# A decoder layer on one core: one table of steps from the opening to the first gate and up products, and 72 products of the output projection behind the last head

## The chip, the cores and the metric

One core of one Trainium2 chip runs the whole layer. The metric is the time of one execution on the device in microseconds (us). The kernel before took 670.38 us, the median of three runs (669.57 to 671.45).

## The reference, cut to what matters

One layer, 512 positions of 1,024 columns, float32:

```
h  = x + rms(mix(rms(x)))                 # sandwich norms around both parts
y  = h + rms(down(silu(gate) * up))       # gate, up = two products of rms(h)

mix: one input projection of rms(x) gives q, k, v of both head groups
  A, 4 heads D0..D3: a = softmax(q1 k1) - lam * softmax(q2 k2);  o = rms(a v)
  B, 8 heads N0..N7 in 2 groups: o = g0 * compressed + g1 * selected + g2 * window
     compressed: 31 blocks of 32 positions, through a small two-layer net
     selected, window: causal softmax over 512 keys
  output projection: concat(A, B) (512 x 1024) times wo (1024 x 1024)
```

The feed-forward part has 2,816 columns, in 22 tiles of 128.

## The kernel before

Every float32 operand of a large product is split in a rounded high part and the rest (whi and wlo, xh and xl, pth and ptl, oh and ol). A product of two such operands is three products on TensorE (PE): high by high, low by high, high by low. ScalarE (ACT) writes most high parts, VectorE (DVE) subtracts most low parts, GpSimd (POOL) some.

The projections (`fm`, `dv`, `vg` in the trace) write q, k and v; q and k go to a scratch in DRAM and come back a head at a time (`qst`, `kst`). A head does, for each of its two maps or branches: score products in three groups of row tiles (`sc`, widths of 128 to 512 columns), maximum on DVE (L510), exponential on ACT (L511), a scaling of the rows (POOL, DVE and ACT, L530 to L534), transposes in three groups (`tr`, L521), high part on ACT (L525), low part on DVE (`ptl`, L526), value products (`av`, `avn`). A differential head (D) then norms its output (`ms`, `rr`, `rs`, `rsb`, L577 to L590). A head of group B (N) adds its compressed branch (`scc`, `pc`, `pcs`, `trc`, `pct`) head by head, in tiles of 128 columns.

The output projection makes four row tiles by two halves of 512 columns, each with three products for each of the eight blocks k of heads: 192 products. `mix_part` (L691) sums the blocks `MIX_A`, which are D0, D1 and N0 to N3, for all four tiles early and parks the sums (`mixp`, 96 products, copied by ACT at L701). `mix_final` (L703) adds the blocks `MIX_B`: for tiles 0 and 1 beside and right behind the last head, for tiles 2 and 3 after that.

Then come the norms (`mixt`, `u`, `x`, a list of short steps `STEPS`, L75, run by `n_step`, L975), their transposes (`trh`, L1020), and the first halves of the first two feed-forward tiles (`gu`, L854), on the rows of tiles 0 and 1. `ff_gate` for the second halves starts when tiles 2 and 3 are normed too; from there on the rest of the feed-forward part (`gw`, L874), the down projection (`acc`, L1166) and the last norm run.

What sets the order: a scheduler places all instructions by simulated times of its own; `ORDER` (L48) is the order in which the projections, heads and weights are written, and heads have a high priority (L545, L549), so that they run above what stands ahead of them. In the norms alone ACT and DVE are held to the written order (`q`, L953). PSUM is split in tags: "mm" 2 banks (projections, mix), "sc" 3 (scores), "tr" 2 (transposes), "av" 1 (values); these are closed behind the heads, and the norms and gates open banks of their own.

Of the kernel before, what the change touches and what calls it, by code (L numbers as in the profile page):

```python
# [46 lines left out]
FIRST_PAIR = {"C": KCVC, "q0": DQ0, "k0": DK0, "n0": NQ0, "s": KSKW, "q1": DQ1, "k1": DK1, "n1": NQ1}  # L47
ORDER = (  # L48
    "C v1 q1 q0 k1 cv n1 W0 k0 n0 ck s v0 g W4 D0 D1 W1 N0 N1 N2 N3 W5 N4 W2 W3 N5 D2 M0 N6 W6 W7 M1 M2 M3 D3 F0 F1 N7"
# [3 lines left out]
PSB = {"mm": 2, "sc": 3, "tr": 2, "av": 1}  # L53
MIX_A = (0, 1, 4, 5)
MIX_B = (2, 3, 6, 7)
# [12 lines left out]
USE_W = "4"  # L68
# [6 lines left out]
STEPS = (  # L75
# [17 lines left out]
def hybrid_block_kernel(  # L93
# [6 lines left out]
    act, dve, pool, pe = nc.scalar, nc.vector, nc.gpsimd, nc.tensor  # L100
# [8 lines left out]
    def load_w(src, w=1024):  # L109
        raw = wpool.tile([P, 1024], F32, tag="raw", name="wraw", bufs=WB[0])  # L110
        nc.sync.dma_start(raw[:, :w], src)
        return raw
# [56 lines left out]
    vcs = T.tile([P, GROUPS, HEAD_DIM], F32R, bufs=1, name="vcs")  # L169
# [18 lines left out]
    nc.sync.dma_start(gc, gcol)  # L188
    xh, xl = [], []
    raws = {}  # L190
    sqs = [None, None]

    def warm(n):
        for j in range(n):
            pe.matmul(warm_ps, warm_b[:, :P], warm_b, start=True, stop=True)

# [3 lines left out]
    warm(WARM)  # L200
# [4 lines left out]
    xraws = [None] * (NK // 2)  # L205

    def load_x(k):
        if k % 2 == 0:
            xraws[k // 2] = T.tile([P, 2, SEQ], F32R, tag="k", name="xraw", bufs=BUFS["k"])
        t = f32(xraws[k // 2][:, k % 2])  # L210
        nc.sync.dma_start(t, xT[:, k])
        h = sslot(f"xh{k}")
        act.activation(h, t, AF.Copy, scale=gc[:, k:k + 1])
        xh.append(h)
        if 0 < k < 4:
            for _ in range(WARMX):
                pe.matmul(warm_ps, h[:, :P], h, start=True, stop=True)

    def low_x(k):
        t = f32(xraws[k // 2][:, k % 2])  # L220
        l = sslot(f"xl{k}")
        dve.scalar_tensor_tensor(l, t, gc[:, k:k + 1], f32(xh[k]), OP.mult, OP.subtract)
        xl.append(l)

    def load_fm(m, split=False):
        raws[m] = load_w(wf[m])
        if split:
            raws[m] = split_w(raws[m])

    first = 2 * FIRST_PAIR[ORDER.split()[0]]  # L230
    load_x(0)
    load_fm(first, True)
    for k in range(1, 4):
        load_x(k)
    load_fm(first + 1, True)
    for k in range(4, NK):
        load_x(k)
    for k in range(NK):
        low_x(k)
    for k in range(NK):  # L240
        t = f32(xraws[k // 2][:, k % 2])
        act.activation(t, t, AF.Square)
        if k < 2:
            sqs[k] = t
        else:
            dve.tensor_tensor(sqs[k % 2], sqs[k % 2], t, OP.add)

    cst = tslot("cst", tag="o")
    nc.sync.dma_start(cst, consts)
    dve.tensor_copy(ident, cst[:, 0:P])  # L250
    dve.tensor_copy(ident_r, cst[:, 0:P])
    dve.tensor_copy(ident_b, cst[:, 0:P])
    dve.memset(mask_b[:, :SEQ - P], 0.0)
    dve.tensor_copy(mask_b[:, SEQ - P:], cst[:, P:2 * P])
    dve.tensor_copy(cmask_b, cst[:, 2 * P:3 * P])
    n2 = GROUPS * NPAD
    dve.tensor_tensor(sel, ident[:, :n2], ident[:, n2:], OP.add)
    for r in (NCMP, n2 + NCMP):
        dve.tensor_tensor(sel, sel, ident[:, r:r + 1].to_broadcast([P, n2]), OP.add)
    dve.tensor_copy(valid, cst[:, 3 * P + 2 * NCMP:3 * P + 2 * NCMP + 1])  # L260
    dve.memset(ones, 1.0)
    zero = T.tile([P, GROUPS], F32, bufs=1, name="zero")
    dve.memset(zero, 0.0)
    rp = [sslot(n, F32) for n in ("cos", "sin", "ckv", "skv")]
    cos, sin, ckv, skv = rp
    for j in range(4):
        nc.sync.dma_start(rp[j], rope[:, j])

    ssum = ps("tr", "ssum")
    for i in range(NT):  # L270
        for j in range(2):
            pe.matmul(ssum[:, i:i + 1], sqs[j][:, i * P:(i + 1) * P], ones, start=(j == 0), stop=(j == 1))
    ssum = ssum[:, :NT]
    rsqrt_mean(rstd, ssum, 1.0 / D_MODEL)
    dve.tensor_scalar_mul(nrstd, rstd, -1.0)
    rb = ps("tr", "rb")
    for i in range(NT):
        pe.matmul(rb[:, i * P:(i + 1) * P], rstd[:, i:i + 1].to_broadcast([P, P]), ident, start=True, stop=True)
    hp = P // 2
    for t in (ckv, skv, cos, sin):  # L280
        dve.tensor_tensor(t, rb, t, OP.mult)

    lv = sslot("lv", F32)
    nc.sync.dma_start(lv[:, :4 * HEAD_DIM], lamv.partition_broadcast(P))
    l2 = T.tile([P, 2], F32, bufs=1, name="l2")
    for j in range(2):
        dve.tensor_tensor(lv[:, 256 + 64 * j:320 + 64 * j], lv[:, 128 * j:128 * j + 64],
                          lv[:, 128 * j + 64:128 * j + 128], OP.mult)
        dve.tensor_reduce(l2[:, j:j + 1], lv[:, 256 + 64 * j:320 + 64 * j], AX.X, OP.add)
    act.activation(l2, l2, AF.Exp)  # L290
    dve.tensor_tensor(lam, l2[:, 1:2], l2[:, 0:1], OP.subtract)
    dve.tensor_scalar_add(lam, lam, -LAM_INIT)


    def fm_tile(m):
        hi, lo = raws.pop(m)
        pt = ps("mm", f"fm{m}")
        seq = [(hi, xh), (lo, xh), (hi, xl)]
        n = 0
        for w, xx in seq:  # L300
            for k in range(NK):
                pe.matmul(pt, w[:, k * P:(k + 1) * P], xx[k], start=(n == 0), stop=(n == 3 * NK - 1))  # L302
                n += 1
        return pt

    def rope_pair(pair, scale, c=None, s=None):
        c = cos if c is None else c
        s = sin if s is None else s
        wide = rope_tile()
        t2, t1, b, a = (f32(wide[:, j]) for j in range(4))  # L310
        for half, outs in enumerate((((t1, c), (a, s)), ((t2, s), (b, c)))):
            m = 2 * pair + half
            if m not in raws:
                load_fm(m, True)
            pt = fm_tile(m)
            if pair == KCVC:
                raw = f32(sslot("craw"))
                act.activation(raw, pt, AF.Copy)
                pt = raw
            for o, tab in outs:  # L320
                dve.scalar_tensor_tensor(o, pt, scale, tab, OP.mult, OP.mult)
        return wide, a, b, t1, t2

    def qk_pair(pair, scale):
        wide, a, b, t1, t2 = rope_pair(pair, scale)
        dve.tensor_tensor(t1, t1, t2, OP.subtract)
        dve.tensor_tensor(a, a, b, OP.add)
        d = dram.tile([4, HALF, 4, SEQ], F32, name=f"qk{pair}")
        hi1, lo1, hi2, lo2 = (wide[:, j] for j in range(4))
        hq = "d" if pair in HIQ else "a"  # L330
        to_r(hq, hi1, t1)
        to_r(hq, hi2, a)
        dve.tensor_tensor(lo1, t1, f32(hi1), OP.subtract)
        dve.tensor_tensor(lo2, a, f32(hi2), OP.subtract)
        nc.sync.dma_start(d.rearrange("m d c t -> (m d) c t"), f32(wide))
        return d

    def load_q(d, m):
        q = T.tile([P, SEQ], F32R, tag="q", name="qst", bufs=BUFS["q"])
        nc.sync.dma_start(f32(q), d[m].rearrange("d c t -> (d c) t"))  # L340
        return q

    def load_k(d, m):
        kk = T.tile([P, 2, SEQ], F32R, tag="k", name="kst", bufs=BUFS["k"])
        src = d[m].rearrange("d (c h) t -> (d c) (h t)", h=2)
        dst = f32(kk).rearrange("(x r) h t -> r x (h t)", r=2)
        for r in range(2):
            nc.sync.dma_start(dst[r], src)
        return kk

    def cmp_pair():
        _, a, b, t1, t2 = rope_pair(KCVC, 1.0, ckv, skv)
        de = f32(rope_tile())[:, :2].rearrange("p x (y n) -> p x y n", y=2)
# [1043 lines left out]
```

## Time and profile before

| what | value |
|---|---|
| time, median of 3 runs | 670.38 us |
| time of the profiled execution | 670.32 us |
| its span in the profile | 668.5 us |
| PE busy | 640.7 us, 96% |
| DVE busy | 559.3 us, 84% |
| ACT busy | 388.6 us, 58% |
| POOL busy | 76.4 us, 11% |

The span is what the profile covers; the time holds 1.8 us around it. A matmul's record lasts until its result has drained, so records of successive products overlap: two products of 0.39 us may start 0.23 us apart, and the spacing is the price of one. "x144" is a count of records, and `128*128 128x512` are the weights' and the moving operand's shape. What stands behind "<-" in brackets is the instruction that ended the wait before a row. In a table of windows the granted clock of PE (1.00 is full) stands behind POOL.

### The profile page before, as it was taken

To read this page: it belongs to the slowest core of one execution; us is meant where nothing else is said; L and a number is where in the kernel's file an instruction comes from. 1 tells how busy PE (TensorE), PEld (TensorE's weight loads), DVE (VectorE), ACT (ScalarE), POOL (GpSimd) and SP (SyncE) were. 2 spreads that over 40 slices of the span, in tenths; PEclk is the share of its full clock that TensorE was granted. 3 is DMA by queue.
4 is the path that set the end of the run, shared out by engine and by line. 5 is a ranking of instruction groups with operands and counts; after the bars stand their busy time and mean duration, and the time that the engine had idled before them with its cause. 6 is when DMAs were issued, how large, how long until landed. Compare 5 with 4: busy or idle time off the path is not lost.

```text
span 668.5 us, 11185 instructions
## 1 busy us (share of the span) xinstructions
PE 640.7 (96%) x4099; PEld 573.1 (86%) x4099; DVE 559.3 (84%) x1114; ACT 388.6 (58%) x820; POOL 76.4 (11%) x86
## 2 busy tenths in 40 slices
PE   8999999999899998888899999999999999999995
PEld 5988788899778787777898999999999998888884
DVE  4878797897999987768999998888888639999966
ACT  6443453657799766635646555555555547665424
POOL 0000000020755532501100000000000000000023
PEclk9999999999999999979989999999999999999998
DMA  8445767771030530136213323323223217562443
GB/s 307 163 142 204 270 223 280 273 284 56 17 127 18 173 104 24 64 106 241 96 64 126 126 97 114 108 96 122 99 95 127 96 49 251 189 219 96 172 112 126
DMA packets 29735, 94.50 MB, mean 141 GB/s; under 512 B 3824, under 2 KB 4720, under 8 KB 28784
## 3 DMA queue, kind: packets, MB, share of 16 engines
q1 hardware_dynamic: 29104, 92.74, 39.5%
q0 software_dynamic: 576, 1.05, 0.9%
q8 instruction: 32, 0.52, 0.3%
q14 instruction: 23, 0.19, 0.1%
HBM read 80.66 MB, written 12.06 MB: 139 GB/s over the span
## 4 chain that ended last, share of the span: by engine, by line
PE 48%; DVE 3%; ACT 1%; issue 1%; DVEq 0%; ACTq 0%
PE gw L874 28%; PE acc L1166 17%; PE gu L854 4%; DVE mixt L958 1%; DVE rr L958 1%; DVE x L958 1%; DVE htl L958 0%; ACT junkb L958 0%; ACT rr L958 0%; ACT hth L958 0%; DVE ug L1073 0%; ACT L859 0%; DVE ffl L1073 0%; DVE cy L930 0%; DVE u L958 0%
## 5 line engine op out<-in xcount | busy, mean ns | idle before, releaser
L530 POOL TENSOR_TENSOR p<-p,l 128x384 f32<-128x384 f32 (+3 forms) x60 | 49.2, 848 | 130.3 <-DVE l L560 57.3
L116 ACT ACTIVATE whi<-wraw 128x1024 fp32r<-128x1024 f32 (+2 forms) x36 | 37.0, 1038 | 44.1 <-PE fm L302 16.0
L511 ACT ACTIVATE p<-p,nm 128x128 f32<-128x128 f32 (+1 forms) x96 | 53.2, 556 | 15.5 <-DVE nm L510 14.9
L126 DVE TENSOR_TENSOR wlo<-wraw,whi 128x1024 fp32r<-128x1024 f32 (+2 forms) x36 | 42.9, 1197 | 18.8 <-ACT whi L116 18.8
L510 DVE CUSTOM_DVE_ANT_0 p<-sc,mask_b 128x128 f32<-128x128 f32 (+1 forms) x96 | 43.9, 483 | 6.5 <-PE sc L506 5.8
L526 DVE TENSOR_TENSOR ptl<-tr,pth 128x384 fp32r<-128x384 f32 (+1 forms) x60 | 35.7, 596 | 5.9 <-ACT pth L525 5.2
L525 ACT ACTIVATE pth<-tr 128x384 fp32r<-128x384 f32 (+1 forms) x60 | 30.9, 517 | 15.4 <-PE tr L521 14.9
L1248 POOL DMA_DIRECT2D rope<-dp x4 | 3.7, 1127 | 315.8 <-DVE rope L1243 315.8
L521 PE MATMUL tr<-ident,p 128*128 128x128 f32 x200 | 34.4, 290 | 3.7 <-DVE rr L139 2.2
L505 PE MATMUL sc<-kst,qst 128*128 128x128 f32 (+2 forms) x96 | 33.5, 357 | 3.9 <-DVE nm L510 2.8
L302 PE MATMUL fm<-xh,whi 128*128 128x512 f32 x128 | 33.5, 396 | 1.2 <-ACT whi L116 1.2
L302 PE MATMUL fm<-xh,wlo 128*128 128x512 f32 x128 | 32.6, 390 | 0.0
L521 PEld LDWEIGHTS tr<-ident,p 128*128 128x128 f32 x200 | 25.2, 149 | 8.6 <-DVE ptl L526 2.9
L302 PE MATMUL fm<-xl,whi 128*128 128x512 f32 x128 | 32.3, 389 | 0.0
L506 PE MATMUL sc<-kst,qst 128*128 128x128 f32 (+2 forms) x96 | 31.0, 326 | 0.0
L302 PEld LDWEIGHTS fm<-xh,whi 128*128 128x128 f32 x128 | 23.6, 188 | 7.0 <-ACT whi L116 1.9
L302 PEld LDWEIGHTS fm<-xl,whi 128*128 128x128 f32 x128 | 24.0, 188 | 5.0
L302 PEld LDWEIGHTS fm<-xh,wlo 128*128 128x128 f32 x128 | 23.8, 188 | 4.8
L505 PEld LDWEIGHTS sc<-kst,qst 128*128 128x128 f32 x96 | 18.5, 193 | 7.7 <-DVE nm L510 6.0
L1073 ACT ACTIVATE ah<-ff 128x256 fp32r<-128x256 f32 (+1 forms) x28 | 14.4, 513 | 14.6 <-DVE ff L1073 11.2
L930 DVE TENSOR_TENSOR cy<-gw,cy 128x512 f32<-128x512 f32 x19 | 13.0, 686 | 11.5 <-PE gw L874 11.5
L874 PE MATMUL gw<-rope,whi 128*128 128x256 f32 x160 | 22.0, 280 | 0.0
(353 smaller groups left out, 2030.3 us busy)
## 6 DMA issues: line engine op xcount, KB each, us to landing
wraw<-in_wg SPq DMA_DIRECT2D x22, 512.0 KB, 3.2
dr<-in_wd SPq DMA_DIRECT2D x22, 512.0 KB, 3.2
wu<-in_wu SPq DMA_DIRECT2D x19, 512.0 KB, 3.2
wraw<-in_wf SPq DMA_DIRECT2D x16, 512.0 KB, 4.7
qk<-rope SPq DMA_DIRECT2D x7, 1024.0 KB, 4.9
kst<-qk SPq DMA_DIRECT2D x24, 256.0 KB, 3.6
qst<-qk SPq DMA_DIRECT2D x16, 256.0 KB, 3.1
wraw<-in_wo SPq DMA_DIRECT2D x8, 512.0 KB, 3.2
```

Of the source, the lines that this page charges most:

```text
L116: act.activation(dst, src, AF.Copy)
L126: (lo_eng or dve).tensor_tensor(lo[:, :w], raw[:, :w], f32(hi[:, :w]), OP.subtract)
L302: pe.matmul(pt, w[:, k * P:(k + 1) * P], xx[k], start=(n == 0), stop=(n == 3 * NK - 1))
L505: pe.matmul(sv, lhs, kk[:, 0, :w], start=True, stop=False)
L506: pe.matmul(sv, lhs, kk[:, 1, :w], start=False, stop=True)
L510: dve.tensor_tensor_reduce(pt, sv, mask_b[:, (NT - 1 - i) * P:], -1.0, BIG, OP.add, OP.min, nm)
L511: act.activation(pt, pt, AF.Exp, bias=nm, scale=-1.0, accum_out=l[:, i:i + 1])
L521: pe.transpose(tr[:, n * P:(n + 1) * P], pts[i][:, j * P:(j + 1) * P], ident)
L526: dve.tensor_tensor(ptl[:, sl], trv, f32(pth[:, sl]), OP.subtract)
L530: pool.tensor_tensor(p, p, l.to_broadcast(list(p.shape)), OP.mult)
L874: m = pe.matmul(pt, ww[:, k * P:(k + 1) * P], hx[k], start=(start and n == 0), stop=(n == 11), skip_group_check=True)
L1166: m = pe.matmul(pt, x, y, start=(start and n == 0), stop=(stop and n == 2), skip_group_check=True)
```

## The change

The instructions from the first load of x to the first halves of the gate products are no longer placed by the scheduler. There are 31 generators ("streams"): loads of x, its high parts, its low parts, weights, projections, evictions, the compression net, scores, maxima, exponentials, scalings, transposes, highs, lows, values, outputs, the differential heads' norms, the output projection's weights, its products, the products behind the last head, four streams of norms, the gates, and so on. A table of 1,543 letters runs the next step of the stream of each letter, and every instruction so issued keeps its written place on its engine:

```diff
-ORDER = (
-    "C v1 q1 q0 k1 cv n1 W0 k0 n0 ck s v0 g W4 D0 D1 W1 N0 N1 N2 N3 W5 N4 W2 W3 N5 D2 M0 N6 W6 W7 M1 M2 M3 D3 F0 F1 N7"
-)
+PROJ = "C v1 q1 k1 cv n1 ck s g q0 k0 v0 n0"
+HEADS = "D2 D3 N4 N5 N6 N7 D0 D1 N0 N1 N2 N3"
+WORDER = "2 3 6 7 0 1 F0 4 5 F1"
+TABLE = (
+    "aaabbcaabbaaPcbPbcbaPaPbaaPbabcPPPPaaccPcPbPbPPPbPPbPcbPPcPdPbdcdPbPPcPbcPSPbcPcPPPPcPPPPcedPPPSSSSeePeP"
...
+    "xxwwwNxNxxNxNWWWWNNNyWWyNyNNzyyzFFyyzFyzyFFzzzzyyyFFyzyzyFzyWzzzzyWFyyzzyyFzzzyyyzFzzFz"
+)
-PSB = {"mm": 2, "sc": 3, "tr": 2, "av": 1}
-MIX_A = (0, 1, 4, 5)
-MIX_B = (2, 3, 6, 7)
+PSB = {"mm": 2, "sc0": 1, "sc1": 1, "sc2": 1, "tr": 2, "av": 1}
+PARK = {1: (2, 3, 6, 7), 2: (2, 3), 3: (2, 3)}
+LATER = {0: (2, 3, 6, 7, 0, 1, 4, 5), 1: (0, 1, 4, 5), 2: (6, 7, 0, 1, 4, 5)}
+LAST_N = 3
+K_LAST = 5
+LATE_PS = {"mix2": ("tr", "tr"), "mix3": ("av", "sc0"), "trh0": ("mm", "mm"), "trh1": ("sc1", "sc2"), "trh2": ("mm", "mm"),
+           "trh3": ("sc1", "sc2"), "gu0": ("tr", "tr"), "gu1": ("av", "sc0")}
-USE_W = "4"
+USE_W = "6"
+    class Written:
+        def __getattr__(self, name):
+            def issue(*a, **k):
+                r = getattr(self.eng, name)(*a, **k)
+                for x in r if isinstance(r, tuple) else (r,):
+                    if self.begun:
+                        tc.keep_in_program_order(x)
+                    self.begun = True
+                return r
+            return issue
+    act, dve, pool, pe, sp = (Written(e) for e in (act, dve, pool, pe, sp))
...
+    need = {t: next(g) for t, g in streams.items()}
+    for t in TABLE:
+        need[t] = next(streams[t], "end")
```

The heads run in the order D2, D3, N4 to N7, D0, D1, N0 to N3; the last block is then k = 5. Row tile 0 parks nothing and sums all its products in PSUM, tile 1 parks the blocks 2, 3, 6, 7, tiles 2 and 3 only 2 and 3. The other six blocks of tiles 2 and 3, 72 products, are a stream (letter N) behind the last head:

```diff
+    def rest():
+        for k in LATER[2]:
+            for i in (2, 3):
+                for c in range(2):
+                    yield [("oh", K_LAST), ("oh", k), ("wo", k)]
+                    if k == LATER[2][0] and not c:
+                        mixes[i] = pair_ps(f"mix{i}")
+                    mix_mul(mixes[i][c], i, c, k, k == LATER[2][0], k == LATER[2][-1])
```

The norms' transposes and the gates use the heads' banks again (`LATE_PS`) and open none of their own. The compressed branch is done for four heads of a group at once, in tiles of 512 columns; the scalings of a head's two branches share one reciprocal and one product with the gates:

```diff
-        def row_scale(b):
-            dve.reciprocal(l[:, b], l[:, b])
-            dve.tensor_tensor(l[:, b], l[:, b], gates[:, :, 3 * h + b], OP.mult)
+                dve.tensor_tensor(l, l, gates[:, :, 3 * h + 1:3 * h + 3].rearrange("p i b -> p b i"), OP.mult)
+                dve.reciprocal(l, l)
-        dve.tensor_reduce(nm, sv, AX.X, OP.max, negate=True)
-        c = T.tile([P, P], F32, tag="pc", name="pc", bufs=2)
+            nm, l = (T.tile([P, nh], F32, tag="nmc", name="nmc", bufs=4) for _ in range(2))
+            dve.tensor_reduce(nm, sv, AX.X, OP.max, negate=True)
+            c = tslot("pc", tag="c")
```

There are 24 loads of `qst` instead of 16, since the compressed scores load their queries apart. The warm products on x are three instead of nine; the products of the first two projections take x in the order of its arrival (`OPEN`). The second feed-forward tile's weights (F1) are split by ACT (high) and POOL (low) instead of DVE, and the norms of the four row tiles are four streams (`NSTEPS`) with the same steps as `STEPS`. From the second halves of the gates on the code is the same.

Two places in PE's program follow. All instructions that the table issues have one line, 230, in the changed kernel; a name's number tells its buffer.

The first place is where the projections end. Before, the last product of the last projection (`vg`) is row 866 of 2,367 of PE's program, with the norm and the scores of a head behind it:

```order
L398 MATMUL vg_1404<-whi,xl_185 128x280
L398 MATMUL vg_1404<-wlo,xh_166 128x280
L398 MATMUL vg_1404<-wlo,xh_169 128x280
L585 MATMUL rsb<-ident,rs 128x128 x4
L505 MATMUL sc<-kst,qst 128x256
L506 MATMUL sc<-kst,qst 128x256
L505 MATMUL sc<-kst,qst 128x512
L506 MATMUL sc<-kst,qst 128x512
L572 MATMUL av<-pth,dv_1212 128x512 x2
L572 MATMUL av<-ptl,dv_1212 128x512
```

In the changed program the last projection (`fm`) ends at row 922 of 2,260, and the head's products stand between its products one by one:

```order
L230 MATMUL fm_2046<-xh_160,wlo 128x512
L230 MATMUL sc<-kst,qst 128x384 x2
L230 MATMUL ms<-ones,sq 128x1 x4
L230 MATMUL tr<-ident,p 128x128 x3
L230 MATMUL av<-pth,vn_1099 128x512
L230 MATMUL av<-ptl,vn_1099 128x512
L230 MATMUL fm_2046<-xh_167,wlo 128x512
L230 MATMUL fm_2046<-xh_173,wlo 128x512
L230 MATMUL fm_2046<-xh_177,wlo 128x512
L230 MATMUL fm_2046<-xh_195,wlo 128x512
```

The first score product moves from row 530 to row 386, so more of the heads' rows stand ahead of the last projection product: before, 140 score, 180 transpose and 172 value products are behind it, after 98, 140 and 139.

The second place is behind the last head, where tiles 2 and 3 of the output projection (`mix`) meet the transposes of the norms of tiles 0 and 1 (`trh`). Before:

```order
L708 MATMUL mix<-ws_2583,oh_3323 128x512
L708 MATMUL mix<-ws_3087,oh_2746 128x512
L708 MATMUL mix<-ws_3087,ol_2747 128x512
L708 MATMUL mix<-ws_3089,oh_2746 128x512
L708 MATMUL mix<-ws_3097,oh_3537 128x512
L708 MATMUL mix<-ws_3097,ol_3538 128x512
L708 MATMUL mix<-ws_3099,oh_3537 128x512
L1020 MATMUL trh<-ident,mixt 128x128 x16
L854 MATMUL gu<-hth,whi 128x256 x16
```

After, in the changed program:

```order
L230 MATMUL mix_3461<-ws_2881,oh_3167 128x512
L230 MATMUL mix_3461<-ws_2881,ol_3168 128x512
L230 MATMUL mix_3461<-ws_2883,oh_3167 128x512
L230 MATMUL trh_3565<-ident,mixt 128x128 x4
L230 MATMUL mix_3462<-ws_2882,oh_3167 128x512
L230 MATMUL mix_3462<-ws_2882,ol_3168 128x512
L230 MATMUL mix_3462<-ws_2884,oh_3167 128x512
L230 MATMUL trh_3566<-ident,mixt 128x128 x4
```

Before, all products of the mix stand ahead of the transposes; after, 39 of the 72 do, and the other 33 stand between and behind the groups of four transposes.

More of the change, by code (lines that the diff above doesn't have):

```diff
@@ L199, in hybrid_block_kernel @@
     warm_ps = ps("av", "warm")
-    warm(WARM)
+    for _ in range(WARM):
+        pe.matmul(warm_ps, warm_b[:, :P], warm_b, start=True, stop=True)
     def rope_tile():
         return R.tile([P, 4, SEQ], F32R, tag="rope", name="rope")
[L205 to L237, printed above, removed]
@@ L273, in hybrid_block_kernel @@
[L273 to L285, printed above, removed]
@@ L306, in rope_pair @@
[L306 to L336, printed above, removed]
+    obj = {}
@@ new lines, in weights @@
+    def weights():
+        todo = [c for tok in PROJ.split()[1:] for c in chunks(tok)]
+        loaded = []
+        for n, (key, src, w) in enumerate(todo):
+            while len(loaded) < min(n + 3, len(todo)):
+                yield ("room", len(loaded))
+                loaded.append(load_w(*todo[len(loaded)][1:]))
+            yield ("room", n)
+            hi, lo = split_slots()
+            act.activation(hi[:, :w], loaded[n][:, :w], AF.Copy)
+            yield
+            dve.tensor_tensor(lo[:, :w], loaded[n][:, :w], f32(hi[:, :w]), OP.subtract)
+            obj[key] = hi, lo
+            obj[("wl",) + key[1:]] = True
@@ new lines, in turned @@
+    def turned():
+        for tok in HEADS.split():
+            if tok[0] == "N":
+                h = int(tok[1])
+                yield ("cgs", h // HPG)
+                tr = ps("tr", "trc", F32R)[:2 * NPAD]
+                for i in range(NT):
+                    b = cgs[h // HPG][h % HPG // 2][:, h % 2 * NT + i].rearrange("p s n -> p (s n)")
+                    pe.transpose(tr[:, i * P:(i + 1) * P], b, ident_r)
+                yield
+                pct = tslot("pct", F32R, "c")[:2 * NPAD]
+                act.activation(pct, f32(tr), AF.Copy)
+                obj["pct", h] = pct
@@ new lines, in hybrid_block_kernel, with transposes @@
+    mats = [(tok, br) for tok in HEADS.split() for br in range(1 if tok[0] == "D" else 2)]
+    def transposes():
+        for mat in mats:
+            for js in GROUPED:
+                yield ("a",) + mat
+                tr, n = ps("tr", "tr"), 0
+                for j in js:
+                    for i in range(j, NT):
+                        pe.transpose(tr[:, n * P:(n + 1) * P], obj[("a",) + mat][i][:, j * P:(j + 1) * P], ident)
+                        n += 1
+                obj["tr", mat, js[0]] = tr[:, :n * P].rearrange("p (j q) -> p j q", q=P)
@@ new lines, in w_col @@
+    def w_col(w, k):
+        if isinstance(w, list):
+            w, k = w[k // 4], k % 4
+        return w[:, k * P:(k + 1) * P]
+    streams = {"a": x_loads(), "b": x_highs(), "c": x_lows(), "d": constants(), "e": row_factors(), "S": weights(), "P": projections(), "R": evictions(), "K": compression(), "G": compressed(), "T": turned(),
+               "Q": loads(), "A": scores(), "X": maxima(), "E": exponentials(), "Y": scalings(), "Z": transposes(),
+               "H": highs(), "L": lows(), "V": values(), "O": outputs(), "J": heads(), "W": out_weights(),
+               "M": mixes_(), "U": parked(),
+               "B": switch(), "N": rest(), "w": norms(0), "x": norms(1), "y": norms(2), "z": norms(3), "F": gates_()}
```

1338 lines of the change are left out of this document (808 added, 530 removed), and 8 rows, old and new, of tables (NSTEPS, STEPS).

## The prediction, made before the changed kernel ran

> **What bounds the kernel now.** I read the page's busy shares first, then a table of windows cut where the program changes stage, then the chain that ended last, and last the PE rows of the weakest window.
>
> ```profile
> PE 640.7 (96%) x4099; PEld 573.1 (86%) x4099; DVE 559.3 (84%) x1114; ACT 388.6 (58%) x820; POOL 76.4 (11%) x86
> ...
> 0.00:20.00 20.00, 18.07 (x69) 11.39 (x70) 10.21 (x23) 13.94 (x22) 0.20 (x4) 1.00 0.85 311
> 20.00:64.00 44.00, 43.77 (x252) 38.33 (x251) 35.50 (x65) 16.77 (x26) 0.00 (x0) 1.00 0.44 142
> 64.00:111.00 47.00, 45.50 (x229) 38.45 (x227) 38.01 (x56) 20.85 (x28) 0.53 (x1) 1.00 0.73 264
> 111.00:164.00 53.00, 52.58 (x373) 49.89 (x374) 44.00 (x112) 32.74 (x87) 4.81 (x6) 1.00 0.62 220
> 164.00:304.00 140.00, 127.50 (x778) 108.74 (x777) 119.51 (x362) 99.80 (x277) 56.94 (x63) 0.96 0.26 84
> 304.00:335.60 31.60, 27.97 (x182) 24.34 (x180) 28.51 (x68) 20.57 (x59) 5.14 (x4) 1.00 0.39 150
> 335.60:550.00 214.40, 213.85 (x1741) 211.15 (x1741) 179.15 (x256) 118.01 (x207) 0.00 (x0) 0.99 0.30 103
> 550.00:668.50 118.50, 111.50 (x485) 90.84 (x485) 104.36 (x180) 65.96 (x117) 8.73 (x8) 0.98 0.49 165
> ```
>
> PE (TensorE) is the bound nearly everywhere. The columns of a window are its length, the busy time of PE, weight load, DVE, ACT and POOL, the granted clock and the DMA. From 335.6 on PE is busy 213.85 of 214.4 us, and nothing the change touches is there: those 332.9 us stay. Before it, two windows are loose: 164 to 304 (the attention heads and the output projection) with 12.5 us without PE, and 304 to 335.6 (the norms and the first gate products) with 3.6. There DVE is the rival bound, at 119.51 of 140 and 28.51 of 31.6.
>
> A busy PE isn't a full one, since records overlap while they drain. So I price products by their spacing:
>
> ```profile
> 335.57 24.34 PE gu L854 x144
> 359.91 187.61 PE gw L874 x1584
> 550.06 111.52 PE acc L1166 x485
> ...
> 283.23 1.05 PE L580 MATMUL ms<-ones,sq 128*128 128x1 f32 x8 [1.26 <-ACT sq L577]
> 292.03 0.34 PE L649 MATMUL avn<-pth,vn 128*128 128x384 f32 x1
> 292.38 0.28 PE L649 MATMUL avn<-pth,vn 128*128 128x256 f32 x1
> 292.61 0.22 PE L649 MATMUL avn<-pth,vn 128*128 128x128 f32 x1
> 292.78 0.40 PE L653 MATMUL avn<-pct,vcs 128*64 128x512 f32 x1
> 293.02 0.49 PE L521 MATMUL tr<-ident,p 128*128 128x128 f32 x3
> 301.94 1.19 PE L708 MATMUL mix<-ws,oh 128*128 128x512 f32 x4 [1.37 <-ACT oh L116]
> 315.68 1.03 PE L1020 MATMUL trh<-ident,mixt 128*128 128x128 f32 x8
> 333.57 0.63 PE L1020 MATMUL trh<-ident,mixt 128*128 128x128 f32 x4 [1.40 <-DVE mixt L958]
> ```
>
> A 512-wide product costs 111.52/485 = 0.230, a 256-wide one 187.61/1584 = 0.118. Two 384-wide ones start 292.03 to 292.38: 0.175 each. Two 128-wide ones start 292.61 to 292.78: 0.085. A score or value product of the heads is a quarter each of these four widths: 0.152. Transposes: 1.03 for eight less 0.63 for four is 0.10; 1.03/8 with the drain is 0.13; I take 0.11. Narrow products: at most 1.05/8 = 0.13; I take 0.115.
>
> Now the weak window by these prices:
>
> ```profile
> L521 PE MATMUL tr<-ident,p 128*128 128x128 f32 x180 | 31.0, 292 | 3.7 <-DVE rr L139 2.2 <-DVE ptl L526 1.5
> L505 PE MATMUL sc<-kst,qst 128*128 128x128 f32 (+2 forms) x70 | 25.1, 368 | 3.1 <-DVE nm L510 2.8
> L649 PE MATMUL avn<-pth,vn 128*128 128x512 f32 (+1 forms) x64 | 20.7, 328 | 0.3 <-DVE opair L661 0.2
> L696 PE MATMUL mixp<-ws,oh 128*128 128x512 f32 x48 | 17.8, 401 | 0.0
> L708 PE MATMUL mix<-ws,oh 128*128 128x512 f32 x30 | 9.9, 399 | 1.4 <-ACT oh L116 1.4
> L598 PE MATMUL scc<-kcl,qst 128*128 128x32 f32 x28 | 6.5, 263 | 0.0
> L585 PE MATMUL rsb<-ident,rs 128*128 128x128 f32 x26 | 4.6, 326 | 1.6 <-DVE rs L146 1.6
> L580 PE MATMUL ms<-ones,sq 128*128 128x1 f32 x24 | 3.0, 245 | 1.3 <-ACT sq L577 1.3
> ```
>
> With the sister rows (L506, L598 and so on are the other parts of a split product), the program has in it 149 512-wide products (mixp 96, mix 45, pct 8) for 34.3 us, 304 score and value products for 46.2, 212 transposes for 23.3 and 106 narrow ones for 12.2: 116 of 140 us. **23.8 us are lost there**, 16% of the time. 5.1 of them are the norm of a differential head (rr 2.2, rs 1.6, sq 1.3), which stands late in the program. From 20 to 164 the same prices leave 3.4 us lost of 144 (2.4%; 2.15 of it idle). From 0 to 20 the 69 products are worth 15.9, so 4.1 are lost. Lost to 304.0 in all: 31.3, and PE's work to there is 272.7.
>
> The Trainium skill's "Perfetto Trace Analysis", section "Identifying the Most-Contended Engine", says that matmul busy time is a poor measure of how near PE is to its limit, and wants weight load's busy share instead. By that share, 86%, 95 us would be free over the whole span. The trace speaks against taking it so here: from 20 to 64 PE runs without a gap at 38.33 of 44, 87%, so that share is what a full PE shows with these products.
>
> **The change, part by part.** *Fewer products.* PE's program is the same but for six warm products fewer (x, 9 to 3): 6 x 0.230 = 1.4. They run while x arrives (DMA 0.85 busy in 0 to 20), so the bounds are 0 and 1.4; I take 1.4, because the new order places real products between the arrivals.
>
> *The output projection's products.* Its 192 products stay. Before, 138 stand ahead of the point where tile 0's mix is done (304.0); after, 114. So 24 x 0.230 = 5.5 leave that part and join the next one.
>
> *Heads beside projections.* The first score product moves from row 530 of PE's program to row 386, and the last projection product from 866 to 922. PE's work by stage is then 71.4 to the first score, 105.8 from there to the last projection, 85.0 on to the last head's values, 3.5 to the join: 265.7. Before, 116 of such work stood with no projection beside it; after, 88.5. This is the main term. Before, heads above projections lose little (0.42 idle of 53 in 111 to 164), because a projection product waits for nothing; so I give the first 176.9 of heads and projections a loss of 3%: 5.3. For the last 88.5 the bounds are 3% and what that window lost without the head's norm, (23.8 - 5.1)/116.2 = 16.1%; the differential heads now stand ahead of four plain heads, and DVE has less to do, but 48 instead of 96 parked products are there to fill gaps. I take halfway, 9.5%: 8.4. With the opening at 4.1, 17.8 are lost instead of 31.3: **13.5 saved.**
>
> *DVE, ACT, POOL, DMA.*
>
> ```profile
> L526 DVE TENSOR_TENSOR ptl<-tr,pth 128x384 fp32r<-128x384 f32 (+1 forms) x54 | 32.1, 595 | 3.6 <-ACT pth L525 3.0
> L118 DVE CAST ws<-wraw 128x512 fp32r<-128x512 f32 x16 | 8.4, 528 | 0.0
> L685 DVE TENSOR_TENSOR ws<-wraw,ws 128x512 fp32r<-128x512 f32 x10 | 7.0, 698 | 0.1
> L631 DVE TENSOR_TENSOR l<-l,gates 128x4 f32<-128x4 f32 x24 | 5.5, 234 | 0.5
> L126 DVE TENSOR_TENSOR wlo<-wraw,whi 128x1024 fp32r<-128x1024 f32 x3 | 3.7, 1225 | 5.3 <-ACT whi L116 5.3
> L685 POOL TENSOR_TENSOR ws<-wraw,ws 128x512 fp32r<-128x512 f32 x6 | 8.7, 1462 | 5.4 <-DVE ws L118 2.9 <-DVE l L631 2.4
> qst<-qk SPq DMA_DIRECT2D x16, 256.0 KB, 3.1
> ```
>
> DVE loses four casts (4 x 0.528, now ACT's), four weight differences (4 x 0.698, now POOL's), and by merging the gates and the compressed branch of four heads about 30 small instructions of 0.234: some 12 us of 119.5. It isn't the bound, so this counts only in the 9.5% above. POOL's four more (4 x 1.462 = 5.8) stand beside 56.94 busy of 140; ACT's four beside 99.80. Eight more query loads go on SP's queue, where DMA is 0.26 busy. The wider compressed products cost PE the same time (0.230 for 512 columns, whichever the rows: 292.78 to the next at 293.02 is 0.24). I count all of these as nothing; should POOL's cover be gone, a weight lands 5.8 late, ahead of products that aren't due until later.
>
> *Behind the last head.* Before: 54 products of the mix (12.4), 32 transposes (3.5), 96 gate products of 256 columns (11.3): 27.2 of the 31.6 us. After: 78 (17.9) + 3.5 + 11.3 = 32.8. Now PE, not DVE (28.51 before; after, one weight split of 1.2 more, L126), is the longer, and 39 of the 72 late products stand ahead of the first transposes, the others between them. The transposes take the old banks of the projections and scores (LATE_PS), last read by evictions that are done by then; if one isn't, it costs one DVE instruction, 0.7. Bounds: 32.8 with no wait, 37.2 with the 4.4 of before. I take half of the last transposes' wait of 1.40, so 33.5: **+1.9.**
>
> *Sum.* -5.5 - 1.4 - 13.5 + 1.9 = -18.5. The execution profiled had a span of 668.5 and a time of 670.32, 1.8 more; the median of the three runs is 670.38, so it stands for them. 668.5 - 18.5 + 1.8 = **651.8**.
>
> ```profile
> 255.00:304.00 49.00, 40.99 (x234) 35.13 (x233) 35.55 (x97) 26.86 (x70) 12.37 (x12) 0.90 0.25 81
> ```
>
> The clock in this last part of the window was granted at 0.90, so 4.9 us of its 49 ran short of clock; they are within the 23.8. The Trainium skill's "TensorE: Matmul & The Clock Gate", section "What's actually happening", says that an idle window of some 3.4 us halves PE's clock. The row agrees in kind: of the windows only the one with the long waits falls below 0.98. By that rule a schedule without long gaps gains these 4.9 wholly, and one with a new gap pays up to 1.7 for each; the sum doesn't rest on it.
>
> **Rivals.** *Filled everywhere.* If the fixed order keeps PE as full in the last 88.5 as beside projections, the loss there is 3%: 4.1 + 8.0 = 12.1 in all, 19.2 saved, 646.1; with no loss but the opening's, 638.1. For it: no engine but PE needs all of that time. Against: before, with 96 products to fill in, 16% was lost.
>
> *The order saves no wait.* If the chains of a head (score, maximum, exponential, scaling, transpose, split, value) set the pace at the end as before, all 31.3 stay and only 5.0 are gained: 665.3. For it: sc waits 2.8 for nm, tr 1.5 for ptl, in a window where DVE is 85% busy. Against: the heads start 144 rows sooner.
>
> *The written order stalls, slower.* Every instruction of the five engines now keeps its place in one table. When DVE's next one has to wait, a split of a transposed group (L526) behind it waits too, and with two banks for transposes PE's next group waits for that. If each of the 60 groups waits for one more DVE instruction, 0.70 as the weight difference, PE loses 42 us beside the 9.4 of opening and projections: 51.4, and the time is 685.4. It decides from (36.3 - 9.4)/60 = 0.45 us a group on, where the time passes 670.3. Against it: all waits for ptl were 1.5 us in the window.
>
> That the change doesn't do what it says is no rival: the order of the program shows it.
>
> **How the numbers follow.** About 0.3%, 2.0 us, can be told from no change. Forecast, 646 to 658: 0.60. Filled everywhere, 638 to 646: 0.13. No wait saved, 658 to 670: 0.16, a quarter of it above 668.3. Stalls, above 670: 0.11, with 0.01 below 672.3. Faster: 0.60 + 0.13 + 0.12 = 0.85; same 0.05; slower 0.10. The range of 641 to 666 leaves out 0.04 below and 0.15 above.
>
> **What would show it.** The first gate products' second halves should start about 317 instead of 335.57, and their chain to the end stay near 333. PE's busy share between the last projection and the join should rise from 0.91 to 0.95 or more, with the clock near 1.00; the opening should stay as long. Wrong: if long waits for ptl, nm or pth grow in the middle (stalls), or if transposes of the norms wait for mixt by more than 3 us in sum (the tail), or if anything behind the gates gets longer.

## The result and the profile after

The changed kernel takes 659.03 us, the median of four runs (658.63 to 661.16), against 670.64 for the kernel before beside it: a ratio of 0.9834, 95% interval 0.9808 to 0.9860. The forecast was 651.8. The execution profiled has a span of 657.0 us, 11.5 less than before (668.5), where 18.5 less was forecast.

The page's first part and a table of windows, cut at the places of the program (the first score product at 82.5, the last projection product at 193.4, the last value product at 285.6, the first product of the second gate halves at 325.2):

```profile
PE 637.2 (97%) x4087; PEld 569.0 (87%) x4087; DVE 546.3 (83%) x1049; ACT 386.5 (59%) x812; POOL 84.0 (13%) x88
...
0.00:20.00 20.00, 17.20 (x70) 10.78 (x71) 13.06 (x25) 13.76 (x20) 0.20 (x4) 1.00 0.82 302
20.00:64.00 44.00, 43.07 (x244) 37.45 (x243) 29.91 (x50) 17.09 (x24) 0.00 (x0) 0.96 0.44 150
64.00:82.50 18.50, 16.34 (x89) 13.29 (x88) 16.80 (x32) 10.03 (x16) 0.53 (x1) 1.00 0.76 253
82.50:193.40 110.90, 107.48 (x674) 95.89 (x673) 90.48 (x222) 65.78 (x172) 19.70 (x21) 1.00 0.50 171
193.40:285.60 92.20, 91.19 (x570) 78.85 (x569) 79.61 (x217) 70.08 (x190) 45.55 (x48) 0.98 0.33 112
285.60:325.20 39.60, 37.85 (x225) 32.24 (x224) 33.88 (x75) 25.83 (x68) 9.30 (x7) 1.00 0.59 226
325.20:657.00 331.80, 324.07 (x2228) 300.50 (x2226) 282.58 (x432) 183.90 (x322) 8.73 (x8) 0.99 0.37 124
```

The loose window of before is gone. Behind the last projection product PE is now idle 1.0 of 92.2 us; before it was 11.1 of 137.3. In its place the program's beginning is looser: 2.8 idle in the first 20 us (1.9 before), a clock of 0.96 in the next 44 (1.00 before), 2.2 idle of the 18.5 up to the first score, 3.4 idle of 110.9 between it and the last projection product. The end of the program, from the second gate halves on, takes 331.8 (332.9 before).

The same path, place by place; the forecast's column is the prediction's sum by stage:

| up to | before | forecast | after |
|---|---|---|---|
| first score product | 111.4 | 77.6 | 82.5 |
| last projection product | 163.0 | 186.6 | 193.4 |
| tile 0's mix done (the join) | 304.0 | 283.5 | 289.4 |
| second gate halves | 335.6 | 317.0 | 325.2 |
| end of the span | 668.5 | 650.0 | 657.0 |

So the forecast was missed by 6.8 us before the last projection product; the heads behind it took 0.9 less than forecast, the tail 2.3 more, the rest 1.2 less. The time lies outside the 646 to 658 to which the prediction gave 0.60, just inside the band of its rival "no wait saved", though waits were saved: behind the last projection PE is busy 0.99 of the time up to the join (94.99 of 96.0 us), where 0.95 or more was forecast.

### The profile page after: what moved, and what is told of

Same layout as the page of the kernel before. It is cut to its first block, busy times and chain, and to the rows that moved or that the text cites. A ratio compares the mean times of both kernels' runs of the same rounds, so it can differ in the third digit from the quotient of the medians.

```text
span 657.0 us, 11063 instructions
## 1 busy us (share of the span) xinstructions
PE 637.2 (97%) x4087; PEld 569.0 (87%) x4087; DVE 546.3 (83%) x1049; ACT 386.5 (59%) x812; POOL 84.0 (13%) x88
## 3 DMA queue, kind: packets, MB, share of 16 engines
q0 software_dynamic: 576, 1.05, 0.9%
## 4 chain that ended last, share of the span: by engine, by line
PE 80%; DVE 10%; DMA 3%; ACT 3%; issue 2%; SPq 0%; DVEq 0%; ACTq 0%
PE gw L1249 27%; PE acc L1464 17%; PE fm L230 9%; PE av L230 4%; PE sc L230 4%; PE v L230 4%; PE mix L230 3%; PE tr L230 3%; PE g L230 2%; PE gu L1232 2%; DMA wraw<-in_wf 2%; PE mixp L230 1%; PE scc L230 1%; DVE rr L230 1%; DMA qk<-rope 1%
## 5 line engine op out<-in xcount | busy, mean ns | idle before, releaser
L230 POOL TENSOR_TENSOR p<-p,l 128x384 f32<-128x384 f32 (+3 forms) x60 | 54.5, 939 | 125.1 <-DVE l L230 100.4
L230 ACT ACTIVATE whi<-wraw 128x1024 fp32r<-128x1024 f32 (+2 forms) x34 | 34.9, 1034 | 24.4 <-issue 13.1
L230 DVE TENSOR_TENSOR wlo<-wraw,whi 128x1024 fp32r<-128x1024 f32 (+2 forms) x34 | 40.8, 1207 | 8.9 <-ACT whi L230 8.9
L230 ACT ACTIVATE pth<-tr 128x384 fp32r<-128x384 f32 (+1 forms) x60 | 30.6, 520 | 25.2 <-PE tr L230 22.7
L230 PE MATMUL sc<-kst,qst 128*128 128x128 f32 (+1 forms) x192 | 41.4, 332 | 1.9 <-DMA kst<-qk 1.6
L230 PE MATMUL fm<-xh,whi 128*128 128x512 f32 x128 | 35.3, 403 | 0.4 <-ACT whi L230 0.4
L230 PE MATMUL fm<-xh,wlo 128*128 128x512 f32 x128 | 34.5, 396 | 0.0
L230 PE MATMUL fm<-xl,whi 128*128 128x512 f32 x128 | 33.5, 392 | 0.0
L230 PEld LDWEIGHTS sc<-kst,qst 128*128 128x128 f32 x192 | 28.8, 190 | 5.1 <-DVE vn L230 2.0
L230 PE MATMUL tr<-ident,p 128*128 128x128 f32 x200 | 31.4, 280 | 1.4 <-DVE ptl L230 1.3
L230 PE MATMUL mix<-ws,oh 128*128 128x512 f32 x84 | 29.6, 403 | 0.0
```

The lines of the kernel that those rows point to most:

```text
L230: r = getattr(self.eng, name)(*a, **k)
```

## The experiments

Each ran five rounds beside the kernel before on one chip, and is compared by its ratio to that, since the chips differ: 0.9834 is "like the changed kernel", and 0.001 is 0.67 us.

### The opening

PE's timeline of the changed kernel and two windows show what became of the first 30 us:

```profile
16.94 0.39 PE L230 MATMUL fm<-xh,whi 128*128 128x512 f32 x1
18.50 0.38 PE L230 MATMUL ssum<-ones,xraw 128*128 128x1 f32 x2 [1.17 <-DVE xraw L230]
19.10 1.72 PE L230 MATMUL ssum<-ones,xraw 128*128 128x1 f32 x14 [0.22 <-DVE xraw L230]
22.21 2.08 PE L230 MATMUL rb<-ident,rstd 128*128 128x128 f32 x8
26.63 0.73 PE L230 MATMUL v<-whi,xh 128*128 128x256 f32 x4 [0.46 <-ACT craw L230]
...
20.00:30.00 10.00, 9.53 (x53) 8.01 (x53) 7.17 (x17) 3.48 (x7) 0.00 (x0) 0.83 0.16 55
21.80:25.20 3.40, 3.39 (x13) 2.80 (x12) 1.41 (x6) 0.00 (x0) 0.00 (x0) 0.50 0.38 130
```

The first v product starts at 26.63; before, at 22.28 with six more warm products. The table has the sums of squares (ssum) ahead of the first projection's last eleven products, and PE waits for DVE there; the eight rb products take 2.08 instead of 1.05. They lie in 3.4 us in which the granted clock was 0.50 (21.8 to 25.2); over the ten from 20 to 30 it was 0.83. The first run moves these steps, and the copies (craw) that free the projections' banks go ahead of the rope tables:

```diff
@@ TABLE, letters 90 to 149 (e: row factors, P: projections, S: weights, R: evictions, r: the new stream) @@
-edPPPSSSSeePePePPPPaaPdSeeeRePPeRRSSRRRPRPPPSRPRSRPRSPPPSRRP
+dPPPSSSSPPPPPPaaPdSRPRePeSeeSPePPPReReeSrrPSPrrSeePPRRrrPrSP
@@ evictions, first_rope @@
+    "r": first_rope()      # the four rope products of the first projection, a stream of their own
```

> The changed kernel with the row factors of the first norm (squares summed on DVE, ssum and rb products, the rope tables) moved behind the first products of v, and the two raw copies of the first projection ahead of them. Theory 1, the opening loses 3 us more than before because PE waits there for the sums (1.3 and 0.4 before ssum, 0.6 before v) and its clock is halved in 21.8 to 25.2: the first v product starts at 23 to 24 instead of 26.6 and the time falls by 2 to 4, to 655 to 657. Rival, the opening is held by x's arrival or by the six missing warm products: the first v product stays above 25.5 and the time within 1 us of 659.

655.73 us, ratio 0.9766 (0.9737 to 0.9794), 4.5 us below the changed kernel. Its timeline has the first v product at

```profile
21.65 0.72 PE L230 MATMUL v<-whi,xh 128*128 128x256 f32 x4
33.19 0.75 PE L230 MATMUL v<-whi,xh 128*128 128x256 f32 x4 [1.66 <-DVE dv L230]
...
20.00:30.00 10.00, 10.00 (x86) 9.95 (x85) 6.38 (x16) 4.33 (x8) 0.00 (x0) 1.00 0.31 107
```

and a full clock in 20 to 30. In the four other runs that leave the opening as it is the first v product starts at 26.3 to 28.3, in the three that have this edit at 21.4 to 22.0. So neither the arrival of x nor the missing warm products were the bound; the place of the sums and copies was. Of the 5.0 us gained at the first v product, 2.0 remain at the last projection product (191.3), since a new wait came in at 33 (a bank waits for dv's low part behind the rope tables on DVE), and 3.1 at the end.

### The middle

Three of PE's waits up to 200 us in the changed kernel (engine and line, what it waited for, us in all, times, longest), and DVE ahead of the last of them:

```profile
PE sc L230 <- DMA kst<-qk: 1.6, 1, 1.6
PE cmp L230 <- DVE rope L230: 1.6, 1, 1.6
PE tr L230 <- DVE ptl L230: 1.3, 1, 1.3
...
148.85 1.23 DVE L230 TENSOR_TENSOR wlo<-wraw,whi 128x1024 fp32r<-128x1024 f32 x1
150.00 0.68 DVE L230 TENSOR_TENSOR ptl<-tr,pth 128x512 fp32r<-128x512 f32 x1
150.74 0.55 PE L230 MATMUL tr<-ident,p 128*128 128x128 f32 x3 [1.35 <-DVE ptl L230]
```

The last three rows are the slower rival's mechanism, at one place: a weight split of 1.23 us stands ahead of a ptl whose high part had been done since 146, and a group of transposes waits.

```diff
-BUFS = {"q": 2, ...
+BUFS = {"q": 3, ...
@@ TABLE @@
 one R (a rope product) from letter 296 to 284; one L (ptl) from letter 600 to 596
```

> The changed kernel with three edits: one rope product on DVE moved ahead of seven instructions so that a bank of the projections is free sooner (PE gap of 1.75 at 77.7), one ptl moved ahead of two DVE instructions (gap of 1.5 at 149), three query buffers instead of two so that SP is not held in front of the key loads (gap of 1.76 at 121.4). Theory 2, these gaps are made by the written order of DVE and SP: they go and the time falls by 3 to 5, to 654 to 656. Rival, whatever stands next in the written order is late too: less than 1 us.

657.85 us, ratio 0.9783 (0.9753 to 0.9812): 3.4 us below the changed kernel, with intervals that just touch. The profile says why it is less than the 4.5 us of the three waits. The wait for the bank (cmp) is gone and that for the keys is 0.4 instead of 1.6, but the next ones in the order take over:

```profile
PE cmp L230 <- DVE wlo L230: 1.7, 2, 1.2
PE tr L230 <- DVE ptl L230: 0.7, 1, 0.7
```

From the first score to the last projection product the stage fell from 110.9 to 109.8 us, behind it up to the last value product from 92.3 to 90.5. Ahead of it nothing was won: the first score comes at 84.5 instead of 82.5, in part because in this execution the first v product, which no edit touches, already started 1.6 us later. So the profiled span is shorter by only 0.3 us (656.7), and the 3.4 rest on the ratios alone.

### The tail

The chain that ended last in the changed kernel, in order of time, shows its long pieces from 297 to the second gate halves:

```profile
297.73 1.67 DVE x L230
303.70 4.81 PE mix L230 x21
308.53 2.05 DVE mixt L230 x3
318.99 1.28 ACT L1222
323.47 1.89 PE gu L230 x16
```

PE ends the late products at 310, and then the norms of tiles 2 and 3 run on DVE and ACT, with PE's gate products beside them. Three runs tried this end. The first turns the order of the 72 products, tile 2 ahead of tile 3:

```diff
-        for k in LATER[2]:
-            for i in (2, 3):
+        for i in (2, 3):
+            for k in LATER[2]:
```

> The changed kernel with the 72 products behind the last head in the order tile 2 first, then tile 3. Theory of the prediction, PE's work bounds the tail: no change, 0 to -0.5 us. Rival, the norms of tiles 2 and 3 on DVE bound its end, because DVE waits 2.0 us for mix at 306.5: tile 2's norm starts 2 us sooner and the time falls by 1 to 2.

659.09 us, ratio 0.9811 (0.9782 to 0.9840): no difference that the intervals tell, and the stretch from the last value product to the second gate halves is the same to 0.03 us (39.58 and 39.55). DVE took two of tile 2's steps at 305.3 and then stood 2.2 us in front of tile 3's, which the table has next. So the second run moves the steps too:

```diff
@@ TABLE (from the 18th late product on; y, z: norms of tiles 2 and 3) @@
-NWWWWNNNyWWyNyNNzyyzFFyyzFyzyFFzzzzyyyFFyzyzyFzyWzzzzyWFyyzzyyFzzzyyyzFzzFz
+NWyyyyyWWWNyNNWWNNNzzFFyyzzFyFzzyyzzyyFFFzyyzzyzzFzzyyyyWWzzFzyyyzzyzFzzFzF
```

> The changed kernel with tile 2's 72 products' half first and the norm steps of tile 2 moved ahead of tile 3's on every engine, since in the run before DVE's wait of 2 us only moved on to tile 3's first step. Rival of the prediction, DVE's chain of the norms of tiles 2 and 3 ends the tail: the last value product to the second gate halves takes 37.5 to 38.5 us instead of 39.7, the time falls by 1 to 2. Theory, PE's work bounds it: 39.5 or more, no change.

660.00 us, ratio 0.9833 (0.9807 to 0.9859). The stretch is 41.1 us instead of 39.6: PE waited for mixt 2.9 us in all at the transposes (1.4 in the changed kernel), of which the earlier place of tile 2's transposes is a part. That DVE's start isn't what counts is not shown by it, since ACT, POOL and the order on PE were changed with it. The third run takes two products with the gain from DVE:

```diff
-    "M0 Q0 M1 Q1 U0/p U1 B L F X0 q0 X1 q1 ...     # tiles 2 and 3
+    "M0 Q0 M1 Q1 U0/p U1/p B L F X0 q0 X1 q1 ...
```

> The changed kernel with one more product with the gain (u) of each of the row tiles 2 and 3 on POOL instead of DVE: 1.4 us less for DVE in the last 15 us of the tail. If DVE's work bounds the end of the tail, the stretch from the last value product to the second gate halves falls from 39.7 to 38.3 to 39 and the time by 0.7 to 1.4. If PE bounds it, no change (39.5 or more); if the chain of one row tile does, it gets longer, since POOL takes 1.3 us for what takes DVE 0.7.

658.92 us, ratio 0.9804 (0.9776 to 0.9832): the same as the changed kernel within the intervals; the stretch got longer, 40.3. It doesn't tell the three bounds apart, since DVE's work did not fall: DVE was busy 34.0 us in it against 33.9, for the rows show something that the edit made worse. It is there in the changed kernel already (timeline of DVE and POOL):

```profile
296.31 0.75 DVE L230 SCALAR_TENSOR_TENSOR x<-u,rr,x 128x512 f32<-128x512 f32 x1
297.73 1.67 DVE L230 SCALAR_TENSOR_TENSOR x<-u,rr,x 128x512 f32<-128x512 f32 x1
317.58 2.47 DVE L230 SCALAR_TENSOR_TENSOR mixt<-x,rr,gain 128x512 f32<-128x512 f32 x2
321.28 1.41 DVE L230 SCALAR_TENSOR_TENSOR mixt<-x,rr,gain 128x512 f32<-128x512 f32 x2
...
297.56 1.29 POOL L230 TENSOR_TENSOR ws<-wraw,ws 128x512 fp32r<-128x512 f32 x1 [10.83 <-ACT ws L230]
317.54 1.30 POOL L230 TENSOR_TENSOR ws<-wraw,ws 128x512 fp32r<-128x512 f32 x1 [5.20 <-ACT ws L230]
```

An x of 0.75 takes 1.67 where POOL subtracts a weight at the same time, and two mixt take 2.47 instead of 1.41. These are the low parts of F1 that the change gave to POOL. The first of them stands in the chain. With two more products on POOL (310.5 to 316.0), in the third run, two x took 2.79 instead of 1.41:

```profile
313.72 2.79 DVE L230 SCALAR_TENSOR_TENSOR x<-u,rr,x 128x512 f32<-128x512 f32 x2
```

### The written order

Now the main term. The first run lets the scheduler place the same instructions:

```diff
-                    if self.begun:
-                        tc.keep_in_program_order(x)
-                    self.begun = True
+                    pass
```

> The changed kernel without the rule that instructions keep their written place on their engine: the scheduler places them by its own times again. If the gain comes from the places that the table gives, the time rises by 5 us or more, to 664 or above. If it comes from what is left out and merged and from the products behind the last head, it stays within 2 us of 659. If the written order stalls the engines (the forecast's slower rival), it falls.

677.23 us, ratio 1.0084 (1.0053 to 1.0115): 17 us above the changed kernel and 5.6 above before. The same instructions, placed by the scheduler, are slower than the kernel before. This is not the kernel before with the merged branch and the late products added: the heads' high priority of before isn't in the changed code, and the scheduler moves the late products too. The windows from the last projection to the last value product and on to the gates, then the mix products behind the last value product here and in the changed kernel, then PE's longest waits:

```profile
191.40:301.70 110.30, 105.28 (x621) 88.17 (x619) 83.08 (x225) 72.48 (x193) 39.44 (x44) 0.98 0.30 101
301.70:340.70 39.00, 29.47 (x168) 26.35 (x167) 29.58 (x71) 24.28 (x66) 8.74 (x6) 0.82 0.44 156
...
301.70:343.00 41.30, 12.49 (x54) 10.07 (x54) 5.02 (x8) 1.37 (x4) 0.83 0.41 147
285.70:326.00 40.30, 22.07 (x93) 17.16 (x93) 5.27 (x8) 1.38 (x4) 1.00 0.58 222
...
PE trh L230 <- DVE mixt L230: 9.5, 2, 4.8
PE sc L230 <- DMA kst<-qk: 4.3, 1, 4.3
```

Up to the last projection product (191.4) this run is 2.0 us ahead of the changed kernel; all that it loses, it loses behind, though its wait for the keys stands ahead of the first score. The scheduler put 39 of the mix products ahead of the last value product, so 54 instead of 93 are left behind it. There PE then waits 9.5 us for the norms' mixt, at a clock of 0.82. How much of the 17 us is the place of these products, and how much the heads' own order, was not tried apart.

Two runs keep the order on a part of the engines:

```diff
-                    if self.begun:
+                    if self.begun and self.eng is nc.tensor:        # a_peonly; "is not" in a_pefree
```

> The changed kernel with the written order kept on PE alone; DVE, ACT, POOL and SP are placed by the scheduler. If the gain of 17 us over the run without any kept order is PE's own order (which product stands beside which), the time stays within 3 us of the changed kernel, a ratio of 0.980 to 0.988. If it is the order of the engines that feed PE, it rises by 8 or more, above 0.995.

> The changed kernel with the written order kept on DVE, ACT, POOL and SP, and PE's instructions placed by the scheduler. If PE's own order carries the gain, the time rises by 8 or more, above 0.995. If the feeding engines' order carries it, PE's products follow it anyway and the time stays within 3 us of the changed kernel, 0.980 to 0.988.

683.75 us (1.0177, 1.0148 to 1.0206) and 691.87 us (1.0294, 1.0267 to 1.0322): both are slower than no kept order at all. Neither PE's order nor the others' carries the gain by itself. With PE's order kept, 93 mix products stand behind the last value product as in the changed kernel, so their place alone doesn't carry it either. With PE's order kept and the feeders placed by the scheduler's times, PE stands in front of what they bring last:

```profile
PE tr L230 <- DVE ptl L230: 5.9, 6, 1.7
PE trh L230 <- DVE mixt L230: 4.8, 2, 3.5
PE ssum L230 <- DVE xraw L230: 3.0, 1, 3.0
```

The first row is the slower rival again, and here it costs: 5.9 us up to the gates, against 1.3 up to 200 us in the changed kernel and none behind.

### Two parts of the change in the kernel before

The first run writes the four differential heads ahead of the others, the second parks three blocks instead of four, so that 60 products instead of 48 stand behind the last head:

```diff
-    "... W4 D0 D1 W1 N0 N1 N2 N3 W5 N4 W2 W3 N5 D2 M0 N6 W6 W7 M1 M2 M3 D3 F0 F1 N7"
+    "... W4 D0 D1 D2 D3 W1 N0 N1 N2 N3 W5 N4 W2 W3 N5 M0 N6 W6 W7 M1 M2 M3 F0 F1 N7"    # b_dfirst
-MIX_A = (0, 1, 4, 5)
-MIX_B = (2, 3, 6, 7)
+MIX_A = (0, 1, 4)                                                                       # b_mix60
+MIX_B = (5, 2, 3, 6, 7)
-USE_W = "4"
+USE_W = "6"                                                                               # b_mix60: the block in the large weight buffers
```

> The kernel before with the four differential heads written ahead of the eight others, scheduler as it was. Theory of the prediction, 5.1 us of the loss at the end of the heads come from a differential head's norm that stands late: the time falls by 3 to 5, to 666 to 668. Rival, the loss at the end comes from the end of the projections as filler, whichever heads stand there, or from the scheduler's own times: within 2 us of before, or slower.

> The kernel before with blocks 0, 1 and 4 parked instead of 0, 1, 4 and 5 (72 parked products instead of 96, 60 behind the last head instead of 48) and the weights of block 6 instead of 4 in the large buffers; nothing else. By the prediction's sums 12 products (2.8 us) leave the part ahead of the join and find room in the tail, where 4.4 of 31.6 were lost: 2 to 3 us faster. Rival, the parked products were what filled PE beside the last heads, or DVE bounds the tail and PE's products delay its transposes: no gain, or up to 3 slower.

Both fell far on the wrong side: 681.46 us (1.0146, 1.0120 to 1.0171) and 685.98 us (1.0211, 1.0185 to 1.0237). The window from the last projection product to the last value product, of before, of the first and of the second run:

```profile
163.00:300.30 137.30, 126.17 (x777) 107.89 (x776) 118.39 (x359) 99.26 (x276) 56.94 (x63) 0.96 0.24 80
163.50:311.40 147.90, 132.19 (x783) 110.92 (x782) 123.86 (x360) 100.63 (x277) 57.22 (x62) 0.94 0.21 69
163.80:313.30 149.50, 131.98 (x757) 111.46 (x756) 121.67 (x357) 101.33 (x274) 57.57 (x63) 0.91 0.22 71
```

With 24 parked products fewer in it (12 of them behind the last head, 12 beside it in the mix) the window got 12 us longer, not shorter: 17.5 us idle instead of 11.1, and a clock of 0.91. With the differential heads early it got 10.6 us longer. The prediction had put 5.1 us of that window's loss down to a differential head's late norm. This run doesn't decide that: the waits for such norms did not go with the early heads, PE still waits for sq and rs 7.3 us in the window. Since the scheduler places every instruction anew at each edit, neither run is the price of its edit alone.

### Together

The edits of the opening (with dv's second low part ahead of the rope tables, where the wait at 33 was), of the middle and of the second tail run, and then without the tail's:

> The changed kernel with the edits of the opening (with one more: the second low part of v ahead of the rope tables, where PE lost 1.8 us at 31 in that run), of the middle and of the tail together. If the losses stand one behind the other on PE's path, the gains add: 3.5 for the opening, 1 to 2 for the middle, 1 to 2 for the tail, so 6 to 7 below the changed kernel, a ratio to before of 0.972 to 0.975. If each only hands the wait on to the next, less than 4 below it (above 0.977).

> The changed kernel with the edits of the opening and of the middle, the tail as in the changed kernel (the turned tail cost 1.4 us more from the last value product on). Expected 1 to 1.5 below the run with all three: a ratio to before of 0.971 to 0.975, 651.5 to 653.5 where before is 670.6. If the turned tail cost nothing, the same as that run, 0.975 or more.

653.84 us (0.9749, 0.9717 to 0.9781) and **653.19 us (0.9727, 0.9701 to 0.9753)**. The second beats both kernels: 7 us below the changed kernel by the ratios, 18 below before. Its span of 651.3 comes out of the same places: last projection product at 189.2 instead of 193.4, last value product at 279.7 instead of 285.65, and the tail unchanged (39.6).

## Why the prediction was right in its direction and 7 us off

**Main term, heads beside projections: right for the end.** The last 88.5 us of work were to lose 9.5%. Priced as there, the stretch from the last projection to the last value product holds 84.1 us of work in 92.3, so 8.2 are lost, 8.9%; before, 24.3 of 137.3. That the size came out so near is partly luck, since 9.5% was taken halfway between two bounds. What the runs add is the cause: of the four ways of placing these instructions that were tried, only the one that holds all engines to the written order gains. The prediction spoke of where heads stand and of DVE's smaller work; without the order the same instructions lose 5.6 us against before.

**The step that failed: "I give the first 176.9 of heads and projections a loss of 3%", and the opening's 4.1.** Up to the last projection product 18.7 us are lost by the same prices instead of 9.4; the time there is 6.8 longer and not 9.3, since by these prices the records hold 174.7 us of work where the sum's stages have 177.2 (71.4 and 105.8; the 176.9 is 0.3 short of them). The opening's first v product comes 4.4 us later than before, because the sums of squares were moved ahead of products that were ready; the run that moves them back gains 5.0 there, of which 2.0 are left at the last projection product. The prediction took from the order only where the first scores and the last projection product went, and held that the opening would stay as long. There are further waits in the written order of DVE and SP, for a bank, for keys and for a ptl. Lifting them gave 1.1 us between the first score and the last projection product, and some came back at the next place. The best run reaches the last projection product at 189.2; 2.6 of the 6.8 us are left there, and what they are stays open.

**The tail: mis-sized.** 33.5 were forecast from the join to the second gate halves, 35.8 measured. PE's products are the 32.8 us of the sum (78 of the mix, 32 transposes, 96 gate products), but 3.0 are lost beside them where the prediction allowed 0.7; PE is idle for 1.75 of these. In the last 15.2 us DVE is busy for 14.45, and the chain that ended last leads through DVE and ACT. That POOL's additional weights cost nothing was wrong there: they lengthened one x by 0.9 us and one pair of mixt by 1.1. The Trainium skill's "SBUF — State Buffer", section "SBUF: two separate sides", says that a DVE operation with two SBUF inputs and a GpSimd operation that reads SBUF exclude each other for a whole instruction. The trace agrees: with both inputs in SBUF an x grows from 0.75 to 1.67 and two mixt from 1.41 to 2.47, and mixt, while it reads the mix from PSUM, stays at 0.68 beside POOL. Whether the tail would end sooner without that work was not tried; what bounds it, PE's sum, DVE's sum or the chain of one tile, stays open.

**Behind the gates: 1.1 better than "unchanged".** Before, the gap ahead of the second gate halves was followed by 3.4 us at half clock:

```profile
336.20:339.60 3.40, 3.40 (x18) 3.40 (x18) 3.40 (x7) 0.00 (x0) 0.00 (x0) 0.51 0.32 123
```

After, the clock is 1.00 from 324 to 335. By an estimate, 3.4 us at half clock cost 1.7, so this is enough for the 1.1 gained (332.9 to 331.8); that it is the whole of it is not shown. The prediction had named this price for a new gap and left it out of the sum.

**The rivals.** Filled everywhere was true only behind the last projection product, in idle time (1.0 of 92.2); by the prediction's prices 8.9% are lost there and not 3%. The stalls of the slower rival exist at a single place, 1.3 us; where PE's order alone was kept they cost 5.9. The six warm products seem spare: in the run with the early v products, these start 0.6 us sooner than before although the sums stand ahead of them, but the order of the first products (`OPEN`) differs there too.

## What to carry to other kernels

A product that is left out or moved is worth its time only if the order around it stays fitted: under a scheduler that places everything anew, writing four heads earlier or moving 12 products behind the last head made this kernel 10 and 14 us slower, and the gain came with an order held on all engines at once. Such an order is to be read engine by engine for instructions that stand ahead of a wait without need: look at each PE wait over 1 us for what its releaser's engine did just before, and move that. Edits at five such places gained 7 us here.

## What the runs showed of the hardware that was not expected

PE's clock was halved without an idle gap. Three windows of the changed kernel, each about 3.4 us:

```profile
212.90:216.40 3.50, 3.50 (x24) 3.11 (x23) 3.46 (x14) 2.67 (x8) 2.18 (x3) 1.00 0.41 116
216.40:219.80 3.40, 3.40 (x26) 3.00 (x25) 3.37 (x10) 2.77 (x8) 0.02 (x1) 1.00 0.41 117
219.80:223.20 3.40, 3.40 (x16) 3.00 (x15) 1.09 (x3) 1.21 (x4) 1.26 (x1) 0.50 0.33 82
```

In the middle one PE's records cover all 3.40 us, but 16 of its 26 products are the compressed scores of 32 columns, now done for four heads together; the next 3.4 us ran at half clock, and 16 products instead of some 25 were issued. The prediction had tied such a halving to an idle window; here none stands ahead of it. In the run with all edits the same stretch did it again, at 215.4; in the six others with the order held it didn't, with the same products, so that the narrow products are the cause is not shown. By an estimate from 3.4 us at half clock it costs 1.7 us. The executions of one kernel also lie apart with their clock: those of the middle's run go from 655.26 us at a mean clock of 0.994 to 658.83 at 0.989, though which stretch was slowed in each isn't on record.
